# A two-layer hybrid block on one core: more weight buffers, earlier small rows, and 256-column products in pairs

## The chip, the cores and the metric

One core of one Trainium2 chip. The metric is the device time of one execution in microseconds. The kernel before was run three times: 1761.48, 1764.64 and 1771.3 us, median 1764.64.

## The reference, cut to what matters

Two layers over 256 latent and 256 context tokens of width 1024 (the context tokens read only context tokens). All arithmetic is float32.

```python
for l in range(2):
    xn = adaln(x, norm1, ...)            # RMS norm, then scale and shift made from c by w_mod
    p  = xn @ w_in                       # columns: cq 384, ckv 256, kr 32, sq 512, sk 128, sv 128,
                                         #          qkv 1536, z 512, a/b 32, gates 3072
    ya = latent attention(cq, ckv, kr)   # 8 heads, w_uq, w_ukv
    yb = window attention(sq, sk, sv)    # 8 heads on 2 key heads, with sinks
    yc = gated DeltaNet, both directions(qkv, a, b) * silu(z)
    y  = (sig(g0)*(ya@w_pa) + sig(g1)*(yb@w_pb) + sig(g2)*(yc@w_pc)) @ w_out
    x  = x + m2 * y
    h  = dwconv(adaln(x, norm2, ...) @ ffn_up); a, b = split(h)
    x  = x + m5 * ((silu(a) * b) @ ffn_down)
return rmsnorm(x, norm_f)
```

In layer 1 the context's outputs are not wanted any more. There cq, sq, z, the gates and all that follows the mixers are computed for the 256 latent tokens alone, while keys and values are still computed for all 512.

## The kernel before, in words

Activations lie transposed in SBUF: features on the partitions, tokens along the free axis, so a product has a 128x128 block of weights as its stationary operand and 512 (layer 0) or 256 (layer 1, latent tokens alone) moving columns. Float32 accuracy comes from two parts. `load_split` (L181) loads up to 512 KB of weights (four row blocks of 256 columns, here called a weight part) into a tile raw, casts it on ACT to a first part wh (L189), and on DVE takes the difference raw - wh as a low part wl (`split_L`, L177). `mm3` (L197) then does three matmuls for each block: wh with the activation's first part, wh with its low part, wl with its first part (L199, L200, L201). The pools have `NRAW` = 3 buffers of raw, `NWH` = 3 of wh and `NWL` = 4 of wl (P, L88 to L93, and L1648). Modulation matrices (`mod_part`, L583) are loaded into raw buffers too, in layer 0's mixers, and used by PE without a split (L593).

`linear` (L274) computes a product in units of 256 output columns, two tiles of 128. A unit takes two PSUM banks (2 KB each, so 512 float32 columns) from the pool mm, which has three, or g, which has five. It goes through the weight parts in order, and within a part through the two column tiles; after the last part each tile is evicted by its own operation.

The order of the work is written by a planner in the kernel. Generators yield estimated microseconds; `chain` (L1391) runs the dependent chains (DeltaNet tables, decay, solve, scan, attention) and after each step `fill` (L214) spends the credit on queued products, the fill work. The queue ends with the gate products (`gates`, L1370): each is evicted through a Sigmoid (L1376), stored to DRAM by a DMA that ACT issues (L1377), and loaded again in the merge (L1515); gates that were not reached ahead are computed in the merge itself (L1531). A scheduler of the framework then orders the instructions of each engine by priority and by buffers that come free. Each engine's queue runs in that order, and an instruction that waits holds up those behind it. Nearly all loads are issued by SP.

`load_vectors` (L538) collects small vectors (biases, norms, convolution taps) as rows of one tile, by nine DMAs, and transposes them on PE. For layer 0 they are issued by POOL at the start, for layer 1 by SP just before layer 0's attention (L1465), where `load_conv` (L561) does the same with the MLP's taps of both layers, by two DMAs each. These use b2 tiles of 2 KB, as the attention does.

Stages of layer 0, about, in us: products for DeltaNet keys 26 to 90, decay, solve and scan to 360, preparation of the attentions to 407, attentions to 510, merge and output product to 700, MLP to 1070. Layer 1: mixers to 1390, attentions to 1470, merge to 1530, MLP to 1750.

Of the kernel before, what the change touches and what calls it, by code (L numbers as in the profile page):

```python
# [14 lines left out]
D = 1024  # L15
# [14 lines left out]
def make_consts():  # L30
# [61 lines left out]
    bx=4, wd=0, dc=1, gk=(0, 0), hpe=60, w_t=5, w_k=3, w_s=0, w_r=1.5, w_n=3, w_o=4.0, nr=3, nh=3, nl=4, nb2=7, st=0, ab=(0.0, 0.0, 0.0, 0.0),  # L92
# [42 lines left out]
class Kernel:  # L135
# [138 lines left out]
    def linear(self, w, k0, nk, c0, ncol, X, evac, cols=None, kgrp=4, split=None, hook=None, gate=False):  # L274
# [5 lines left out]
        for u0 in range(0, ncol, 256):  # L280
# [5 lines left out]
            pss = [self.ps([128, T], "g" if self.wide and self.unit % 2 else "mm") for _ in range(nt)]  # L286
# [11 lines left out]
            def products(kg, wt, cs):  # L298

                g, H, L = wt  # L300
                for i in range(nt):
                    due = g
                    for k in range(g):
                        cc = slice(i * 128, i * 128 + 128)
                        self.mm3(pss[i][:, cs[i]], H[:, k, cc], L[:, k, cc], XH[kg + k][:, cs[i]], XL[kg + k][:, cs[i]],
                                 kg + k == 0, kg + k == nk - 1)
                        if hk:
                            hk["n"] += 1
                            if hk["n"] in self.P["hk"]:
                                next(hk["g"])  # L310
                        elif k % self.P["ly"] == self.P["ly"] - 1 and k < g - 1:
                            yield (cs[i].stop - cs[i].start) * self.P["ly"] * 3 / 2400
                            due -= self.P["ly"]
                    if kg + g == nk:
                        with self.tc.high_priority(self.P["hpe"]):
                            evac(u0 // 128 + i, pss[i], cs[i])
                    yield (cs[i].stop - cs[i].start) * due * 3 / 2400
# [13 lines left out]
            cs = [cols(u0 // 128 + i) if cols else slice(0, T) for i in range(nt)]  # L331
            for kg in range(0, nk, kgrp):
                yield from products(kg, load(kg), cs)
# [204 lines left out]
    def load_vectors(self, l):  # L538

        nc, i = self.nc, self.ins  # L540
        q = nc.gpsimd if l == 0 else nc.sync
        ident = self.con("ident")
        rows = self.b2([128, 128])
        for nm, (r0, n) in VEC_ROWS.items():
            if nm == "gdn_norm":
                for h in range(2):
                    q.dma_start(out=rows[r0:r0 + 1, h * 64:h * 64 + 64], in_=i[nm][l:l + 1, :])
                continue
            a = i[nm] if nm == "norm_f" else i[nm][l]
            if nm == "gdn_conv":  # L550
                a = a.rearrange("t (r c) -> (t r) c", c=128)
            else:
                a = a.rearrange("(r c) -> r c", c=128)
            q.dma_start(out=rows[r0:r0 + n, :], in_=a)
        for a, b in ((0, 56), (56, NVEC)):
            yield
            ps = self.ps([128, T], "g")
            nc.tensor.transpose(ps[:, :b], rows[:b, :], ident[:b, :b])
            nc.vector.tensor_copy(self.vec[l][:, a:b], ps[:, a:b])

    def load_conv(self, l):  # L561
# [735 lines left out]
    def layer(self, l):  # L1297
# [25 lines left out]
        def proj_cq():  # L1323
            cq = A["cq"] = self.b4([128, 3, n]) if last else self.s8([128, 3, n])
            yield from self.linear(w, 0, KD, C_CQ, 384, X, lambda t, p, cs: self.evac(t, cq[:, t, :], p[:, cs]), cols=c_o)
# [6 lines left out]
        def proj_sq():  # L1332
# [4 lines left out]
            for u in range(2):  # L1337
                self.gsync()
                pss = [self.ps([128, T], "mm") for _ in range(2)]
                for kg in range(0, KD, 4):  # L1340
# [6 lines left out]
                    H, L = self.load_split(pieces, [128, 4, 256])  # L1347
                    for j in range(2):
# [6 lines left out]
                    yield 5.1 * len(streams) / 2  # L1355

        def proj_z():
            if not last:
                A["zs"] = self.s8([128, 4, n])
            zs = A["zs"]  # L1360

            def evz(t, p, cs):
                nc.scalar.activation(out=zs[:, t, :], in_=p[:, cs], func=AF.Silu)

            yield from self.linear(w, 0, KD, C_Z, 512, X, evz, cols=c_o)
# [4 lines left out]
        def gates():  # L1370

            for bi, (gi, _) in enumerate(gate_br):
                for u in range(4):
                    def ev(t, p, cs, bi=bi, u=u):
                        sg = self.b2([128, T])[:, :n]
# [4 lines left out]
                    yield from self.linear(w, 0, KD, C_GATE + gi * D + u * 256, 256, X, ev, cols=c_o, gate=True)  # L1380
# [339 lines left out]
```

## Time and profile before

| | |
|---|---|
| runs | 1761.48, 1764.64, 1771.3 us; median 1764.64 |
| profiled execution | 1760.08 us, its span 1758.3 us |
| mean granted TensorE clock | 0.976 |
| busy: PE / PE's weight loads / DVE / ACT / POOL | 95% / 77% / 66% / 44% / 12% |
| instructions | 31525 |
| HBM read, written | 213.85 MB, 11.80 MB; mean 130 GB/s |

PE is TensorE's matmuls, PEld its weight loads, DVE VectorE, ACT ScalarE, POOL GpSimd, SP SyncE. A q behind an engine's name marks its sequencer, which issues DMAs. L and a number is a line of the kernel. `out<-in` names tiles without their buffer numbers. An arrow in brackets behind an idle time names what ended it.

### The profile page before, as it was taken

Reading aid. Unit: us, or ns where it says so; the run is one execution under the profiler, and the core shown is the slowest. Engines: PE = TensorE matmul, PEld = TensorE weight load, DVE = VectorE, ACT = ScalarE, POOL = GpSimd, SP = SyncE. Lnnn points to the kernel's source line nnn. Section 1 sums busy time; section 2 is a strip of 40 time slices with the busy share of each in tenths; the row PEclk is TensorE's granted clock in tenths of the full one; section 3 lists DMA queues with packets and bytes.
Section 4 is the critical chain, followed back from the end, with each engine's and each line's share of the span. In section 5 each row is a group of like instructions: output and inputs, shape, how many; then the busy total and the mean of one; then the engine's idle time right before and its main releaser. Section 6 shows DMA issues by size and latency. Waiting matters only on the chain. (4 is left out here: it accounts for less than half of the span.)

```text
span 1758.3 us, 31525 instructions
## 1 busy us (share of the span) xinstructions
PE 1668.4 (95%) x12723; PEld 1355.3 (77%) x12723; DVE 1160.7 (66%) x2223; ACT 777.4 (44%) x1377; POOL 217.0 (12%) x217
## 2 busy tenths in 40 slices
PE   6989998998999999999999999989988899999997
PEld 3768766775557888668888888778887667999997
DVE  3888697675775534545435553699997877667684
ACT  3664412234665233324324433465532575556463
POOL 1000000002100312011001111020302301212010
PEclk9999998998999999999999999999897999999999
DMA  9424335333135533853233343434351223745663
GB/s 348 118 59 122 103 100 172 74 87 101 55 102 175 185 124 105 313 186 101 87 105 96 96 157 109 126 90 132 103 130 38 61 85 107 235 145 178 185 186 123
DMA packets 216944, 228.75 MB, mean 130 GB/s; under 512 B 51228, under 2 KB 195422, under 8 KB 215646
## 3 DMA queue, kind: packets, MB, share of 16 engines
q1 hardware_dynamic: 211582, 220.11, 40.9%
q10 hardware_dynamic: 4928, 6.56, 1.0%
q8 instruction: 100, 1.64, 0.4%
q14 instruction: 46, 0.38, 0.1%
q0 software_dynamic: 288, 0.06, 0.0%
HBM read 213.85 MB, written 11.80 MB: 128 GB/s over the span
## 5 line engine op out<-in xcount | busy, mean ns | idle before, releaser
L179 DVE TENSOR_TENSOR wl<-raw,wh 128x1024 fp32r<-128x1024 f32 (+2 forms) x294 | 357.7, 1217 | 236.9 <-ACT wh L189 235.7
L189 ACT CAST wh<-raw 128x1024 fp32r<-128x1024 f32 (+2 forms) x294 | 298.6, 1018 | 382.3 <-PE mm L200 187.6
L199 PE MATMUL mm<-xnh,wh 128*128 128x512 f32 (+2 forms) x1072 | 378.6, 354 | 4.6 <-DVE s L131 1.9
L201 PE MATMUL mm<-xnh,wl 128*128 128x512 f32 (+2 forms) x1072 | 373.2, 351 | 5.0 <-DVE wl L179 4.9
L200 PE MATMUL mm<-xnl,wh 128*128 128x512 f32 (+2 forms) x1072 | 374.4, 350 | 0.0
L199 PEld LDWEIGHTS mm<-xnh,wh 128*128 128x128 f32 (+1 forms) x1072 | 204.8, 191 | 39.2 <-issue 7.7
L201 PEld LDWEIGHTS mm<-xnh,wl 128*128 128x128 f32 (+1 forms) x1072 | 204.3, 191 | 35.6 <-DVE wl L179 7.0
L200 PEld LDWEIGHTS mm<-xnl,wh 128*128 128x128 f32 (+1 forms) x1072 | 204.8, 191 | 27.6 <-issue 4.0
L199 PE MATMUL g<-xnh,wh 128*128 128x256 f32 (+1 forms) x496 | 167.6, 340 | 1.4 <-ACT xnh L405 1.4
L200 PE MATMUL g<-xnl,wh 128*128 128x256 f32 (+1 forms) x496 | 166.3, 337 | 0.2 <-DVE xnl L406 0.2
L201 PE MATMUL g<-xnh,wl 128*128 128x256 f32 (+1 forms) x496 | 166.3, 337 | 0.0
L199 PE MATMUL mm<-s,wh 128*128 128x256 f32 (+1 forms) x458 | 149.4, 328 | 0.7 <-DVE s L534 0.6
L201 PE MATMUL mm<-s,wl 128*128 128x256 f32 (+1 forms) x458 | 149.3, 327 | 0.6 <-DVE wl L179 0.6
L200 PE MATMUL mm<-s,wh 128*128 128x256 f32 (+1 forms) x458 | 149.1, 326 | 0.1
L1620 POOL TENSOR_TENSOR b<-b,b 128x512 f32<-128x512 f32 (+1 forms) x44 | 54.4, 1237 | 442.1 <-DVE b L1604 381.1
L199 PEld LDWEIGHTS g<-xnh,wh 128*128 128x128 f32 x496 | 94.7, 192 | 15.0 <-issue 3.3
L201 PEld LDWEIGHTS g<-xnh,wl 128*128 128x128 f32 x496 | 94.7, 191 | 10.5 <-issue 1.2
L199 PE MATMUL g<-s,wh 128*128 128x512 f32 (+1 forms) x304 | 102.7, 338 | 0.0
L200 PEld LDWEIGHTS g<-xnl,wh 128*128 128x128 f32 x496 | 94.7, 191 | 10.1 <-DVE xnl L406 0.8
L200 PE MATMUL g<-s,wh 128*128 128x512 f32 (+1 forms) x304 | 102.2, 336 | 0.0
L201 PE MATMUL g<-s,wl 128*128 128x512 f32 (+1 forms) x304 | 102.1, 336 | 0.0
L199 PEld LDWEIGHTS mm<-s,wh 128*128 128x128 f32 x458 | 86.8, 190 | 8.8 <-DVE s L534 1.1
(290 smaller groups left out, 2699.0 us busy)
## 6 DMA issues: line engine op xcount, KB each, us to landing
raw<-in_w_in_dram SPq DMA_DIRECT2D x92, 512.0 KB
raw<-in_ffn_up_dram SPq DMA_DIRECT2D x80, 512.0 KB
s<-in_w_mod_dram SPq DMA_DIRECT2D x64, 512.0 KB
raw<-in_w_mod_dram SPq DMA_DIRECT2D x32, 512.0 KB
raw<-in_ffn_down_dram SPq DMA_DIRECT2D x32, 512.0 KB
raw<-in_w_out_dram SPq DMA_DIRECT2D x16, 512.0 KB
raw<-in_ffn_down_dram SPq DMA_DIRECT2D x16, 384.0 KB
spill<-s SPq DMA_DIRECT2D x4, 1024.0 KB
```

The costliest lines, as they stand in the source:

```text
L179: self.nc.vector.tensor_tensor(out=out, in0=x, in1=h.bitcast(F32), op=ALU.subtract)
L189: nc.scalar.copy(H, raw)
L199: mm(ps, lhsT=wH, rhs=xH, start=start, stop=False)
L200: mm(ps, lhsT=wH, rhs=xL, start=False, stop=False)
L201: mm(ps, lhsT=wL, rhs=xH, start=False, stop=stop)
L1620: nc.gpsimd.tensor_tensor(out=y[:, cs], in0=y[:, cs], in1=av[t][:, cs], op=ALU.mult)
```

## The change

It raises `nr` (raw) from 3 to 5 and `nh` (wh) from 3 to 4, and makes room for that by a smaller scratch area for the descriptors of POOL's DMAs. It issues layer 1's small rows and the taps of both layers on SP right after layer 0's spill of x, into row buffers of their own; their transposes stay where they were. In layer 1 the products of cq, sq, z and the gates that are computed ahead use one PSUM bank per unit: two tiles of 256 columns side by side. For that all weight parts of a unit are loaded and split first, then the first column tile is accumulated through all parts, then the second, and one operation evicts both; a gate unit is stored by one DMA in place of two. The gates computed in the merge, the MLP and layer 0's products keep two banks.

```diff
-    ... nr=3, nh=3, nl=4, nb2=7 ...
+    ... nr=5, nh=4, nl=4, nb2=7 ...
...
-    def linear(self, w, k0, nk, c0, ncol, X, evac, cols=None, kgrp=4, split=None, hook=None, gate=False):
+    def linear(self, w, k0, nk, c0, ncol, X, evac, cols=None, kgrp=4, split=None, hook=None, gate=False, pair=False):
...
-            pss = [self.ps([128, T], "g" if self.wide and self.unit % 2 else "mm") for _ in range(nt)]
+            tag = "g" if self.wide and self.unit % 2 else "mm"
+            if pair:
+                bank = self.ps([128, 2, S], tag)
+            else:
+                pss = [self.ps([128, T], tag) for _ in range(nt)]
...
-                    if kg + g == nk:
+                    if kg + g == nk and (not pair or i == nt - 1):
                         with self.tc.high_priority(self.P["hpe"]):
-                            evac(u0 // 128 + i, pss[i], cs[i])
+                            if pair:
+                                evac(u0 // 128, bank[:, :nt], cs[i])
+                            else:
+                                evac(u0 // 128 + i, pss[i], cs[i])
...
+            if pair:
+                wts = [(kg, load(kg)) for kg in range(0, nk, kgrp)]
+                for i in range(nt):
+                    for kg, wt in wts:
+                        yield from products(kg, wt, cs, (i,))
+                continue
...
-        rows = self.b2([128, 128])
+        rows = self.b2([128, 128]) if l == 0 else self.sb([128, 128], "rows", F32, 3)
+        if l:
+            self.rows = rows
+            for j in range(DEPTH):
+                q.dma_start(out=rows[NVEC + 4 * j:NVEC + 4 * j + 4, :], in_=i["ffn_conv"][j].rearrange("t (r c) -> (t r) c", c=128)[128:132, :])
...
-        f0, f1 = self.b2([128, 128]), self.b2([128, 128])
+        f0, n = self.sb([128, 128], "rows", F32, 3), NVEC + 4 * DEPTH
         nc.sync.dma_start(out=f0, in_=fr[0:128, :])
-        nc.sync.dma_start(out=f1[:4, :], in_=fr[128:132, :])
+        yield
         ps = self.ps([128, T], "g")
         nc.tensor.transpose(ps[:, :128], f0, ident)
-        nc.tensor.transpose(ps[:, 128:132], f1[:4, :], ident[:4, :4])
-        nc.vector.tensor_copy(self.fcv[l], ps[:, :132])
+        nc.tensor.transpose(ps[:, 128:128 + n], self.rows[:n, :], ident[:n, :n])
+        nc.vector.tensor_copy(self.fcv[l][:, :128], ps[:, :128])
+        nc.vector.tensor_copy(self.fcv[l][:, 128:132], ps[:, 128 + NVEC + 4 * l:132 + NVEC + 4 * l])
...
                     def ev(t, p, cs, bi=bi, u=u):
+                        if last:
+                            sg = self.b2([128, 2, S])
+                            nc.scalar.activation(out=sg, in_=p, func=AF.Sigmoid)
+                            nc.scalar.dma_start(out=gate_in[:, bi, 2 * u:2 * u + 2], in_=sg)
+                            gate_n[1] += 1
+                            return
...
+        if l == 0:
+            small = [self.load_vectors(1)] + [self.load_conv(j) for j in range(DEPTH)]
+            for g in small:
+                next(g)
...
-            for _ in self.load_vectors(1):
-                pass
-            for j in range(DEPTH):
-                self.load_conv(j)
+            for g in small:
+                for _ in g:
+                    pass
...
-    nc = bacc.Bacc("TRN2", target_bir_lowering=False, num_devices=1)
+    nc = bacc.Bacc("TRN2", target_bir_lowering=False, num_devices=1, dynamic_dma_scratch_size=2048)
```

`proj_cq`, `proj_z` and `gates` pass `pair` in layer 1; `proj_sq` does the same by hand, with its four matmul blocks of a part kept until both column tiles are through. cq and sq alternate between ACT and DVE by unit where they did by tile.

## Rows read from the trace of the kernel before

**Rows 1.** The page, busy time of the engines (share of the span, instructions).

```profile
PE 1668.4 (95%) x12723; PEld 1355.3 (77%) x12723; DVE 1160.7 (66%) x2223; ACT 777.4 (44%) x1377; POOL 217.0 (12%) x217
```

**Rows 2.** Waits of PE, whole run: total us, times, longest us.

```profile
PE mm L593 <- DMA raw<-in_w_mod_dram: 6.6, 6, 2.8
...
PE mm L201 <- DVE wl L179: 5.6, 5, 3.5
...
PE mm L199 <- DVE s L131: 1.9, 1, 1.9
...
PE mm L199 <- ACT wh L189: 0.9, 1, 0.9
```

**Rows 3.** Stretches: length, busy us (instructions) by engine, granted clock, DMA share, GB/s.

```profile
core 0: us, PE busy (x) PEld busy (x) DVE busy (x) ACT busy (x) POOL busy (x), PEclk, DMA share, GB/s
110.00:121.00 11.00, 7.45 (x32) 5.26 (x32) 10.93 (x14) 6.70 (x9) 1.04 (x2) 1.00 0.14 49
121.00:125.00 4.00, 4.00 (x12) 3.12 (x11) 2.82 (x21) 0.45 (x1) 0.00 (x0) 0.57 0.48 131
...
250.00:267.00 17.00, 13.87 (x275) 8.67 (x274) 15.16 (x44) 0.60 (x1) 0.00 (x0) 1.00 0.69 230
267.00:272.00 5.00, 4.61 (x82) 3.20 (x83) 3.26 (x7) 1.41 (x4) 0.00 (x0) 0.66 0.80 273
...
414.00:425.00 11.00, 9.55 (x36) 5.42 (x37) 5.09 (x19) 4.28 (x11) 0.93 (x1) 0.53 0.55 178
...
1144.00:1320.00 176.00, 162.43 (x1804) 143.21 (x1804) 166.01 (x331) 90.41 (x153) 32.80 (x31) 0.96 0.43 112
...
1500.00:1540.00 40.00, 40.00 (x336) 40.00 (x335) 24.77 (x33) 21.59 (x33) 10.25 (x10) 1.00 0.72 238
```

**Rows 4.** PE in order of time, 384 to 425 us: start, us, instruction [idle before].

```profile
413.04 0.64 PE L593 MATMUL mm<-raw,cT 128*32 128x256 f32 x8 [2.82 <-DMA raw<-in_w_mod_dram]
...
414.95 0.42 PE L558 MATMUL g<-cst,b 114*128 114x114 f32 x1 [1.07 <-DMA b<-in_gdn_norm_dram]
...
416.55 0.45 PE L570 MATMUL g<-cst,b 128*128 128x128 f32 x1 [0.38 <-DVE fcv L572]
```

**Rows 5.** SP in order of time, whole run, equal issues merged.

```profile
3.06 0.60 SPq L186 DMA_DIRECT2D raw<-in_w_in_dram  x1
3.70 15.89 SPq L458 DMA_DIRECT2D s<-in_w_mod_dram  x14
...
44.42 28.08 SPq L186 DMA_DIRECT2D raw<-in_w_in_dram  x7
...
395.86 12.72 SPq L591 DMA_DIRECT2D raw<-in_w_mod_dram  x2
408.62 0.44 SPq L554 DMA_DIRECT2D b<-in_b_mod_dram  x1
...
415.19 0.25 SPq L568 DMA_DIRECT2D b<-in_ffn_conv_dram  x1
```

**Rows 6.** Waits of ACT, whole run.

```profile
ACT wh L189 <- PE mm L200: 187.6, 87, 7.9
```

**Rows 7.** Waits of SP's queue, whole run.

```profile
SPq L591 <- PE mm L593: 95.5, 18, 26.1
```

**Rows 8.** DVE in order of time, 112 to 121 us.

```profile
115.14 3.93 DVE L131 STREAM_TRANSPOSE s<-s 32x1024 f32<-32x1024 f32 x2
...
119.18 1.22 DVE L179 TENSOR_TENSOR wl<-raw,wh 128x1024 fp32r<-128x1024 f32 x1
```

**Rows 9.** ACT's groups by form, whole run: count, busy us, mean ns, idle before.

```profile
L1376 ACT ACTIVATE b<-mm 128x512 f32<-128x512 f32 x16 | 9.5, 597 | 12.4 <-PE mm L201 11.4 <-PE g L939 1.0
...
L1376 ACT ACTIVATE b<-mm 128x256 f32<-128x256 f32 x18 | 6.6, 382 | 5.8 <-PE mm L201 5.7
```

**Rows 10.** DMA issues: count, KB each, median us to landing.

```profile
b<-in_norm_dram POOLq DMA_DIRECT2D x2, 4.0 KB, 5.4
```

**Rows 11.** PE in order of time, 44 to 50 us.

```profile
45.28 0.26 PE L558 MATMUL g<-cst,b 114*128 114x114 f32 x1
```

More of the change, by code (lines that the diff above doesn't have):

```diff
@@ L91 @@
     lag=(0, 0, 2, 4, 5), nmod=(2, 5), hk=(5, 12), f0=(1.0, 1.6, 1.0, 1.0, 1.5, 1.0, 1.0), f1=(1.0, 1.0, 1.0, 0.3, 1.0, 1.0, 0.3), lat=1.0,
-    bx=4, wd=0, dc=1, gk=(0, 0), hpe=60, w_t=5, w_k=3, w_s=0, w_r=1.5, w_n=3, w_o=4.0, nr=3, nh=3, nl=4, nb2=7, st=0, ab=(0.0, 0.0, 0.0, 0.0),
+    bx=4, wd=0, dc=1, gk=(0, 0), hpe=60, w_t=5, w_k=3, w_s=0, w_r=1.5, w_n=3, w_o=4.0, nr=5, nh=4, nl=4, nb2=7, st=0, ab=(0.0, 0.0, 0.0, 0.0),
     st2=6, bge=2, hpa=40, hpn=0, hpk=40, hpv=40)
@@ L296, in load, with products @@
                 return (g,) + self.load_split(pieces, [128, g, uw])
-            def products(kg, wt, cs):
+            def products(kg, wt, cs, tiles=None):
                 g, H, L = wt
-                for i in range(nt):
+                for i in tiles or range(nt):
                     due = g
@@ L304, in products @@
                         cc = slice(i * 128, i * 128 + 128)
-                        self.mm3(pss[i][:, cs[i]], H[:, k, cc], L[:, k, cc], XH[kg + k][:, cs[i]], XL[kg + k][:, cs[i]],
+                        self.mm3(bank[:, i] if pair else pss[i][:, cs[i]], H[:, k, cc], L[:, k, cc], XH[kg + k][:, cs[i]], XL[kg + k][:, cs[i]],
                                  kg + k == 0, kg + k == nk - 1)
@@ L1324, in proj_cq @@
             cq = A["cq"] = self.b4([128, 3, n]) if last else self.s8([128, 3, n])
-            yield from self.linear(w, 0, KD, C_CQ, 384, X, lambda t, p, cs: self.evac(t, cq[:, t, :], p[:, cs]), cols=c_o)
+            if last:
+                yield from self.linear(w, 0, KD, C_CQ, 384, X, lambda t, p, cs: self.evac(t // 2, cq[:, t:t + p.shape[1], :], p), cols=c_o, pair=True)
+                return
+            yield from self.linear(w, 0, KD, C_CQ, 384, X, lambda t, p, cs: self.evac(t, cq[:, t, :], p[:, cs]))
         def alloc_zsq():
@@ L1338, in proj_sq @@
                 self.gsync()
-                pss = [self.ps([128, T], "mm") for _ in range(2)]
+                pss = [self.ps([128, T], "mm") for _ in range(1 if last else 2)]
+                wts = []
                 for kg in range(0, KD, 4):
@@ L1347, in proj_sq @@
                     H, L = self.load_split(pieces, [128, 4, 256])
+                    if last:
+                        wts.append((H, L))
+                        continue
                     for j in range(2):
@@ L1354, in proj_sq @@
                             self.evac(j, sq[:, 2 * u + j, :], pss[j][:, oc])
-                    yield 5.1 * len(streams) / 2
+                    yield 5.1
+                for j in range(2 if last else 0):
+                    for k in range(KD):
+                        H, L = wts[k // 4]
+                        self.mm3(pss[0][:, j * S:j * S + S], H[:, k % 4, j * 128:j * 128 + 128], L[:, k % 4, j * 128:j * 128 + 128],
+                                 XH[k][:, oc], XL[k][:, oc], k == 0, k == KD - 1)
+                    if j:
+                        self.evac(u, sq[:, 2 * u:2 * u + 2, :], pss[0].rearrange("p (j c) -> p j c", j=2))
+                    yield 2.56
         def proj_z():
@@ L1362, in evz @@
             def evz(t, p, cs):
-                nc.scalar.activation(out=zs[:, t, :], in_=p[:, cs], func=AF.Silu)
-            yield from self.linear(w, 0, KD, C_Z, 512, X, evz, cols=c_o)
+                nc.scalar.activation(out=zs[:, t:t + 2, :] if last else zs[:, t, :], in_=p if last else p[:, cs], func=AF.Silu)
+            yield from self.linear(w, 0, KD, C_Z, 512, X, evz, cols=c_o, pair=last)
         gate_in, gate_br = self.dram.tile([128, 3, 8, n], F32, name=f"gates{l}"), ((2, "c"), (0, "a"), (1, "b"))
@@ L1374, in ev @@
                     def ev(t, p, cs, bi=bi, u=u):
+                        if last:
+                            sg = self.b2([128, 2, S])
+                            nc.scalar.activation(out=sg, in_=p, func=AF.Sigmoid)
+                            nc.scalar.dma_start(out=gate_in[:, bi, 2 * u:2 * u + 2], in_=sg)
+                            gate_n[1] += 1
+                            return
                         sg = self.b2([128, T])[:, :n]
@@ L1379, in gates @@
                     gate_n[0] += 1
-                    yield from self.linear(w, 0, KD, C_GATE + gi * D + u * 256, 256, X, ev, cols=c_o, gate=True)
+                    yield from self.linear(w, 0, KD, C_GATE + gi * D + u * 256, 256, X, ev, cols=c_o, gate=True, pair=last)
         def push(*gens):
```

## The prediction

> **What bounds the kernel now.** I read the page first, for the busiest engine: PE is busy 1668.4 of 1758.3 us [rows 1], so all that can be had without removing matmuls is 1758.3 - 1668.4 = 90 us of idle time, plus what slow clock costs. The change removes no matmul. Second, the waits of PE over the whole run, to see which of that idle time a deeper supply of weights could end. Four rows matter [rows 2]: 6.6 us for the modulation matrices (tile raw), 5.6 us for the low halves wl, 1.9 us and 0.9 us before the first matmul of a product. The other waits of PE are for links of the DeltaNet and softmax chains, which the change does not touch. Third, the table of stretches around the longest of these waits [rows 3]: after each of them the granted clock of the next few microseconds is 0.57, 0.66 and 0.53 of full speed, that is, mostly the lower of the two levels, 1.2 GHz. A wait costs its idle time and a slow stretch behind it. Fourth, the queues that feed PE: ACT's wait list says that the cast to wh is held up mostly by PE's last use of an older wh, 187.6 us in 87 waits [rows 6]; SP's says that modulation loads wait 95.5 us for PE to give back a raw buffer [rows 7]. So wh and raw are the short buffers; idle time there costs PE nothing until it surfaces in [rows 2].
>
> **Part 1: five raw and four wh buffers.** Taken by stretch, against the profiled execution (1758.3 us span, 1760.08 us in all).
>
> (a) Start of the layer-0 attention. SP issues one modulation load at about 396 us and the next only when PE has freed a buffer, just before 408.62; PE starts on it at 413.04, after 2.82 us idle [rows 4, 5]. With two more buffers that load goes out with the earlier ones. Then PE waits 1.07 us for the small rows and 0.38 us behind their eviction [rows 4]; with the rows loaded 370 us earlier the first goes, and the second goes too, as the four transposes no longer wait for loads one by one. Idle: 2.82 + 1.07 + 0.38 = 4.3. In 414 to 425 us PE is busy 9.55 us at clock 0.53 [rows 3]; at full clock that is 9.55 x 0.47 = 4.5 us less. I take 4.0, since some of the drop may come anyhow. DVE is busy only 5.09 of those 11 us, so nothing else bounds. Sum 8.3.
>
> (b) Layer-0 scan, 250 to 272 us. The other raw waits are 6.6 - 2.8 = 3.8 us [rows 2, 4], and the slow stretch after them costs 4.61 x 0.34 = 1.6 us [rows 3]. But DVE is busy 15.16 of 17 us there: PE that arrives sooner will partly wait for the scan's next DVE result. That is what is late next. I take half of 5.4: 2.7.
>
> (c) wl. Its longest wait, about 3.5 us, has its reason in DVE's order: the split stands behind 3.93 us of stream transposes and starts at 119.18 [rows 2, 8]. With a fourth wh the cast, and so the split, can be ordered a weight part earlier. Idle 5.6 us, slow clock 4.00 x 0.43 = 1.7 us [rows 2, 3], together 7.3. DVE has 10.93 of 11 us full there, but what PE waited with was fill work that nobody's chain needs. I take two thirds: 4.9.
>
> (d) The 0.9 us for wh [rows 2] is in the dense layer-0 MLP: 0.9.
>
> DVE and ACT do as many casts and splits as before.
>
> **Part 2: early small rows.** Thirteen SP issues leave 408.62 to 415.44 us, where they cost the above, for the place behind the spill, before the raw loads at 44.42 us [rows 5]. They take SP up to 6.8 us there. PE and ACT do not stand behind them: only the weight loads do, and those seven loads spend 28.08 us at SP because raw buffers are full [rows 5], so the delay is covered as long as three (now five) parts lie ahead. Bounds 0 to +6.8; I take 0, nearest to that row. Two small evictions for one per layer on DVE: under 1 us beside other work, 0. The rows' own 512-byte buffers free five b2 tiles at the attention's start: 0.
>
> The descriptor scratch shrinks to 2048 bytes. The trace shows no wait for it. Nine row loads on POOL land up to 5.4 us after issue [rows 10]; one after another from 1.3 us they would end near 50, and PE wants the last at 45.28 [rows 11]: bounds 0 to +4.6. They are small and now overlap, so 0. At the start one raw load goes ahead of fourteen modulation loads that take 15.89 us, 1.14 each [rows 5]; two more raw buffers may let two more ahead: 0 to +2.3. The order of the first is kept by the queue, not by lack of buffers, so 0.
>
> **Part 3: pairs in layer 1.** Gates done ahead (18 evictions, so 9 units), z, cq and sq, 2 units each: 15 units. Matmuls stay. A Sigmoid takes 382 ns on 256 columns and 597 on 512 [rows 9]: 9 x (2 x 382 - 597) = 1.5 us off ACT, and 9 fewer stores, all off the path. A unit takes one of three mm banks instead of two, which can end the 1.9 us wait for an evicted bank [rows 2]. Against it, the first column tile must be finished before the second starts, so the second weight part is wanted after half a column tile's products. PE does 336 matmuls in 40 us in a full stretch [rows 3], 0.119 us each; a part of one tile is 12 of them, 1.43 us, where until now both tiles' 24, 2.86 us, came first. Between: -1.9 to +15 x 1.43 = +21.5 us. I take -1.0: casts and splits run ahead of PE, and the waits for wl are 5.6 us in the whole run, of which 3.5 us are one wait in layer 0 [rows 2].
>
> Here the Trainium skill speaks against the change: "PSUM — Partial Sum Buffer", section "The four PSUM rules", says that two accumulation groups open in one bank spoil each other when the second starts, so a shared bank forces the groups one after the other. No row here shows two in one bank; if every unit paid for that order in full, the sum would be 16.8 - 21.5, a loss of 4.7 us.
>
> **Sum:** 8.3 + 2.7 + 4.9 + 0.9 + 1.0 = 17.8 us. The profiled execution lies 4.6 us (0.26%) under the median of 1764.64, so 1742 for its like, and 1764.6 - 17.8 = 1747 for the median.
>
> **Rivals.** *The buffers only park more loads.* A modulation load keeps its buffer until PE uses it, and SP is one queue: five full buffers block it like three. For it: 95.5 us of such waits [rows 7], and DVE full beside (b) and (c). Against: in (a) one more buffer is all that is missing. Then only (a) stays, 4.3 to 8.3 us: 1756 to 1760, say 1758, no change that shows. A measurement of this kernel tells about 0.5% (8.8 us) from none.
>
> *Slower: the pairs starve PE.* Place: the layer-1 stretch 1144 to 1320 us, where DVE is busy 166.01 of 176 us [rows 3]. There a split that is wanted 1.43 us sooner is not made sooner, since wl stays at four buffers and DVE has no room. Price: per unit 1.43 us if it just comes late, or about 3.5 plus 1.7 of slow clock if it falls behind a transpose, as in (c). With eight of the units in that stretch at 3.9 on average, 31 us against the 16.8 of the other terms and more: 1764.6 + 15 = 1780. It decides from (16.8 + 8.8) / 8 = 3.2 us a unit on. Against: wh, the shorter buffer, gets deeper.
>
> *More than forecast.* Casts that wait for PE hold ACT's queue [rows 6], and with it the Exp and Square that chains stand behind. In 1144 to 1320 us PE idles 176 - 162.43 = 13.6 us and loses 162.43 x 0.04 = 6.5 to the clock [rows 3]; with two thirds of these 20 gone, 1747 - 13 = 1734. Against: DVE, not ACT, is full there.
>
> **How the numbers follow.** Forecast 0.48, parked loads 0.24, pairs starve 0.13, more 0.15. The forecast's own bounds: all of (a) to (d) and the bank wait, 8.8 + 5.4 + 7.3 + 0.9 + 1.9 = 24, gives 1740; the costs of part 2, 6.8 + 4.6 + 2.3, would take most of the gain back: 1761. The range runs from half of the "more" case, 1733, over parked loads to 1766; outside lie the starved pairs and some of "more", 0.2. Faster: 0.15 and all but 0.01 of 0.48, 0.62; same 0.25; slower 0.13.
>
> **What would show it.** Right: the waits for raw and wl in PE's list fall from 12.2 us to under 4; in the attention's first 15 us there is no modulation or row wait, and its clock is 1.0; modulation loads wait for PE as long as before, but two loads further ahead. (b) is wrong if the scan's waits for DVE grow by what raw gives back. Part 3 is right if L201's waits in layer 1 stay under 1 us, and wrong if they come near 10. Part 2 is wrong if the first 80 us get longer. The whole is wrong if the layer-0 waits are gone and the span is not shorter: then the chains set it.

## The result, and the profile after

The change makes the kernel faster: 1742.05 us, the median of four runs (1739.98 to 1744.14), against 1767.97 us for the kernel before on the same chip (1761.48 to 1773.14); ratio 0.9863, 95% interval 0.9839 to 0.9886. The profiled execution of after spans 1738.9 us. That of before (1758.3, its own time 1760.08) lies below all the timed runs of before, so the profiles differ by 19.4 us where the medians differ by 25.9. All that follows accounts for the 19.4.

The page of after, busy time (answers to [rows 1]), and the waits of PE over the whole run (answers to [rows 2]; total us, times, longest us; L955 is now L974, L593 L612, L1098 L1117):

```profile
PE 1663.4 (96%) x12723; PEld 1356.9 (78%) x12723; DVE 1162.7 (67%) x2224; ACT 771.9 (44%) x1360; POOL 211.1 (12%) x217
```

```profile
PE g L974 <- DVE b L963: 7.8, 8, 1.5
...
PE mm L201 <- DVE wl L179: 2.8, 2, 2.3
...
PE mm L612 <- DMA raw<-in_w_mod_dram: 2.2, 4, 0.8
...
PE g L1117 <- ACT s L194: 2.0, 1, 2.0
```

The waits for raw and wl are down from 12.2 to 5.0 us, and 2.3 of these 5.0 are one new wait. The wait for DVE in the scans of both layers (L974) has grown from 5.0 to 7.8 us; by windows it fell in layer 0's scan, from 3.5 to 3.0, and rose in layer 1's, from 1.5 to 4.9.

Where the 19.4 us went is read from the table of stretches, with the same six stages cut in both kernels: to the last scan product of layer 0 (A), to the last value product of its attention (B), to the last residual after its MLP (C), to layer 1's last scan product (D), its last value product (E), and the end (F). Columns are the stretch, its length, busy time and instructions of PE, PEld, DVE, ACT, POOL, granted clock, DMA share, GB/s. Before:

```profile
0.00:354.10 354.10, 325.07 (x3222) 243.52 (x3222) 258.06 (x534) 140.06 (x241) 14.09 (x25) 0.98 0.45 136
354.10:551.90 197.80, 185.44 (x1038) 121.86 (x1032) 135.26 (x375) 114.54 (x270) 21.33 (x25) 0.96 0.32 95
551.90:1098.00 546.10, 544.24 (x2771) 441.71 (x2770) 259.97 (x350) 186.05 (x263) 74.48 (x61) 1.00 0.43 141
1098.00:1364.30 266.30, 242.32 (x2856) 210.10 (x2857) 228.82 (x459) 121.17 (x217) 42.21 (x39) 0.94 0.39 103
1364.30:1476.80 112.50, 102.53 (x659) 71.76 (x655) 84.01 (x213) 71.11 (x155) 18.73 (x22) 0.98 0.24 71
1476.80:1758.30 281.50, 268.77 (x2199) 266.31 (x2197) 194.60 (x294) 144.50 (x232) 46.13 (x45) 0.98 0.57 175
```

After:

```profile
0.00:351.50 351.50, 325.90 (x3221) 245.00 (x3221) 258.48 (x535) 138.57 (x240) 14.10 (x25) 0.97 0.46 141
351.50:541.60 190.10, 183.22 (x1042) 121.41 (x1037) 134.84 (x377) 114.20 (x270) 20.92 (x25) 0.97 0.31 100
541.60:1084.20 542.60, 541.26 (x2767) 441.10 (x2766) 260.86 (x350) 185.96 (x263) 75.84 (x61) 1.00 0.43 140
1084.20:1350.60 266.40, 243.55 (x2859) 210.75 (x2858) 228.66 (x458) 117.63 (x204) 41.18 (x39) 0.93 0.39 106
1350.60:1458.60 108.00, 101.33 (x655) 72.66 (x650) 84.25 (x212) 70.64 (x153) 18.51 (x22) 0.97 0.25 74
1458.60:1738.90 280.30, 268.14 (x2199) 266.04 (x2197) 195.57 (x293) 144.93 (x231) 40.52 (x45) 0.98 0.55 171
```

PE's instructions are the same stage by stage to within four (a few records are missing, and a few matmuls move across a cut), so the lengths may be compared: A gains 2.6 us, B 7.7, C 3.5, E 4.5, F 1.2, and D loses 0.1. The gain around the start of layer 0's attention is as forecast. The first 81 us are longer, and layer 1's attention is shorter; neither was in the sum.

### The profile page after: what moved, and what is told of

It reads as the page before. It is cut to its first block, busy times and chain, and to the rows that moved or that the text cites. A ratio compares the mean times of both kernels' runs of the same rounds, so it can differ in the third digit from the quotient of the medians.

```text
span 1738.9 us, 31515 instructions
## 1 busy us (share of the span) xinstructions
PE 1663.4 (96%) x12723; PEld 1356.9 (78%) x12723; DVE 1162.7 (67%) x2224; ACT 771.9 (44%) x1360; POOL 211.1 (12%) x217
## 4 chain that ended last, share of the span: by engine, by line
PE 77%; DVE 13%; issue 4%; DMA 3%; ACT 2%; POOL 0%; SPq 0%; POOLq 0%; DVEq 0%; ACTq 0%
PE mm L199 13%; PE mm L200 12%; PE mm L201 12%; PE g L199 8%; PE g L200 8%; PE g L201 8%; DVE s L131 3%; PE g L1070 2%; PE g L1133 2%; DVE wl L179 2%; PE g L1117 2%; DMA s<-in_w_mod_dram 2%; DVE sm L131 1%; PE g L612 1%; PE g L974 1%
## 5 line engine op out<-in xcount | busy, mean ns | idle before, releaser
L199 PE MATMUL mm<-xnh,wh 128*128 128x512 f32 (+2 forms) x1072 | 378.8, 355 | 4.6 <-DVE s L131 2.0
L1663 POOL TENSOR_TENSOR b<-b,b 128x512 f32<-128x512 f32 (+1 forms) x44 | 49.6, 1128 | 444.1 <-DVE b L1647 391.8
```

The costliest lines, as they stand in the source:

```text
L199: mm(ps, lhsT=wH, rhs=xH, start=start, stop=False)
L1663: nc.gpsimd.tensor_tensor(out=y[:, cs], in0=y[:, cs], in1=av[t][:, cs], op=ALU.mult)
```

## The experiments

Twelve kernels: first each part alone, then parts taken out of the change, then the pairs taken apart. The table has the length of each stage in us, from windows cut at the same instructions as above, and the time against the kernel before on the same chip.

| kernel | A | B | C | D | E | F | median us | ratio to before, 95% |
|---|---|---|---|---|---|---|---|---|
| before | 354.1 | 197.8 | 546.1 | 266.3 | 112.5 | 281.5 | | |
| after | 351.5 | 190.1 | 542.6 | 266.4 | 108.0 | 280.3 | 1742.05 | 0.9863 (0.9839 to 0.9886) |
| 1 buffers alone | 346.4 | 199.3 | 542.9 | 266.3 | 121.1 | 280.5 | 1758.26 | 0.9966 (0.9950 to 0.9982) |
| 2 early rows alone | 352.7 | 190.6 | 546.4 | 265.7 | 116.0 | 281.5 | 1754.72 | 0.9949 (0.9924 to 0.9974) |
| 3 pairs alone | 353.5 | 199.9 | 546.3 | 271.6 | 112.1 | 281.2 | 1766.20 | 1.0022 (0.9999 to 1.0046) |
| 4 no pairs | 353.4 | 189.8 | 542.6 | 268.7 | 118.3 | 280.4 | 1753.19 | 0.9940 (0.9918 to 0.9962) |
| 5 no early rows | 347.1 | 200.2 | 542.3 | 266.6 | 108.2 | 280.3 | 1746.74 | 0.9902 (0.9884 to 0.9920) |
| 6 raw 5, wh 3 | 353.9 | 189.9 | 545.2 | 268.8 | 114.9 | 281.0 | 1754.71 | 0.9947 (0.9927 to 0.9966) |
| 7 raw 3, wh 4 | 355.3 | 196.4 | 541.4 | 264.7 | 107.9 | 280.9 | 1748.10 | 0.9896 (0.9870 to 0.9922) |
| 8 rows later | 346.9 | 191.6 | 542.4 | 267.4 | 107.9 | 280.5 | 1738.47 | 0.9856 (0.9834 to 0.9878) |
| 9 two evictions | 351.0 | 190.1 | 542.3 | 267.9 | 107.2 | 280.1 | 1740.37 | 0.9861 (0.9833 to 0.9888) |
| 10 order, two banks | 351.7 | 192.8 | 542.2 | 272.7 | 113.8 | 280.0 | 1752.10 | 0.9924 (0.9899 to 0.9949) |
| 11 gates unpaired | 350.6 | 190.0 | 542.9 | 273.8 | 113.5 | 280.4 | 1752.19 | 0.9925 (0.9900 to 0.9951) |
| 12 rows later, wh 5 | 350.3 | 190.6 | 539.9 | 275.6 | 111.5 | 283.7 | 1746.80 | 0.9896 (0.9869 to 0.9923) |

A row of stages is one execution. After and runs 4, 9, 10 and 11 have the same code up to layer 1, and their A, B and C spread over 2.8, 3.0 and 0.7 us, so a smaller difference in one stage shows nothing. The profiled executions of runs 12, 10 and 4 lie 6.6, 2.9 and 1.8 us above their medians, that of before 4.3 us below its median beside runs 1 to 4 (1764.39): the verdicts rest on the ratios.

### Each part alone

**Run 1, the buffers alone** (against before):

```diff
-    ... nr=3, nh=3, nl=4 ...
+    ... nr=5, nh=4, nl=4 ...
-    nc = bacc.Bacc("TRN2", target_bir_lowering=False, num_devices=1)
+    nc = bacc.Bacc("TRN2", target_bir_lowering=False, num_devices=1, dynamic_dma_scratch_size=2048)
```

> The kernel before with five raw and four wh buffers (and the smaller descriptor scratch that makes room), nothing else. Theory (the buffers carry the gain): 12 to 20 us faster than before; layer 0's scores start 7 to 13 us earlier, since the 2.82 us modulation wait and most of the slow clock behind it go while the 1.07 us row wait stays; the wl waits at 115 to 121 us go; the tables end where they ended before. Rival 'parked loads': 4 to 8 us, all of it at the start of layer 0's attention. Rival 'the pairs bring the late gain': what is gained by the end of layer 1's scan is all there is, so the attention and merge of layer 1 take as long as before.

Measured: ratio 0.9966, about 6 us, the size that the parked loads would give, but not in their place. A gains 7.7 us and C 3.2; B, where the forecast had its largest term, gains nothing; E loses 8.6. At the attention's start PE still waits 1.7 us for a modulation load and 1.4 us for the rows. PE's row there (start, length, ..., [idle before <- what ended it]) and SP's timeline (start, length, operation, count) show why:

```profile
405.07 0.64 PE L593 MATMUL mm<-raw,cT 128*32 128x256 f32 x8 [1.68 <-DMA raw<-in_w_mod_dram]
```

```profile
363.50 19.45 SPq L591 DMA_DIRECT2D raw<-in_w_mod_dram  x5
...
400.55 0.33 SPq L591 DMA_DIRECT2D raw<-in_w_mod_dram  x1
400.92 0.43 SPq L554 DMA_DIRECT2D b<-in_b_mod_dram  x1
...
407.58 2.46 SPq L591 DMA_DIRECT2D raw<-in_w_mod_dram  x5
```

The load that PE waits for is the sixth. Five had gone out from 363.50 us on and filled the five buffers; the sixth went out at 400.55 us, after SP had waited 17.0 us for PE to give a buffer back. That is what the parked loads would do. Five more loads then stand behind the rows, 6.6 us in SP's queue, but PE waits for none of them: the 1.7 us are all its waiting for modulation in B.

**Run 2, the early rows alone** (against before, which keeps three buffers each; the scratch is as in after):

```diff
+        if l == 0:
+            small = [self.load_vectors(1)] + [self.load_conv(j) for j in range(DEPTH)]
+            for g in small:
+                next(g)
...
-            for _ in self.load_vectors(1):
-                pass
-            for j in range(DEPTH):
-                self.load_conv(j)
+            for g in small:
+                for _ in g:
+                    pass
```

> The kernel before with the small rows issued early (and the smaller scratch), three raw and three wh buffers, no pairs. Theory: the thirteen early issues hold up the weight loads behind them, so the tables end 2.6 to 7 us later (worse than the 2.6 us with five raw buffers); the row wait of 1.07 us and the 0.38 us behind it go at the attention's start, where the 2.82 us modulation wait stays. In all 1 us faster to 5 us slower. Rival (my own forecast, rows cost nothing): 0 to 3 us faster, the first 90 us unchanged.

Measured: about 9 us faster, beyond what either side expected. B is 190.6 us, as in after, with three raw buffers. So most of the gain at the attention's start is the rows': run 1 has the buffers and not the gain, run 2 the gain and not the buffers. But part of the modulation wait stays with three raw, in run 2 and in run 7 below, and is nearly gone in after (PE's rows of run 2, run 7 and after):

```profile
412.01 0.64 PE L598 MATMUL mm<-raw,cT 128*32 128x256 f32 x8 [1.36 <-DMA raw<-in_w_mod_dram]
```

```profile
414.70 0.64 PE L612 MATMUL mm<-raw,cT 128*32 128x256 f32 x8 [1.50 <-DMA raw<-in_w_mod_dram]
```

```profile
410.60 0.62 PE L612 MATMUL mm<-raw,cT 128*32 128x256 f32 x2 [0.25 <-DMA raw<-in_w_mod_dram]
```

In all of these, before and run 1 included, the load waited for is the one that SP could issue only when PE had given back its first modulation buffer (at 408.25, 400.55, 406.93, 409.48 and 405.66 us in before, runs 1, 2, 7 and after), and PE goes on 4.5 to 5.2 us after that issue. What differs is how long PE has other work before it wants the load: 2.0 us in before, 2.8 in run 1, 3.7 in runs 2 and 7, 4.7 in after. Two more buffers give it two more loads to multiply with, some 0.9 us. With early rows it does their transposes and the first scores in that time, some 1.8 us, where in run 1 these stand behind the wait.

**Run 3, the pairs alone** (against before: `pair` in `linear`, `proj_cq`, `proj_sq`, `proj_z` and `gates` as in the change, nothing else).

> The kernel before with the pairs alone, three raw and three wh buffers. Theory: nothing changes until layer 1; its mixers take 2 us less to 4 us more, the total is within 4 us of before. Rival 'pairs starve PE': 10 to 30 us slower, with waits for wl of 10 us or more in 1144 to 1320 us, since here no deeper wh helps. Rival 'the pairs bring the late gain': layer 1's attention and merge take about 6 us less and the total is 4 to 8 us less.

Measured: 1.0022, no change that shows. D takes 5.3 us more, E 0.4 less. Neither starved to a price of 10 us nor a gain of 6.

**Run 4, after without the pairs** (against after):

```diff
-                    yield from self.linear(w, 0, KD, C_GATE + gi * D + u * 256, 256, X, ev, cols=c_o, gate=True, pair=last)
+                    yield from self.linear(w, 0, KD, C_GATE + gi * D + u * 256, 256, X, ev, cols=c_o, gate=True)
...
```

with the same for cq, sq and z.

> The kernel after without the pairs (buffers and early rows stay). Theory: within 2 us of the kernel after, so about 22 to 27 us faster than before. Rival 'pairs starve PE': 2 to 10 us faster than the kernel after, as the 1.6 us that layer 1's mixers lost come back. Rival 'the pairs bring the late gain': 4 to 8 us slower than the kernel after, lost in layer 1's attention and merge.

Measured: 0.9940, so 0.8% slower than after, most of it in E (118.3 against 108.0). The theory fell. Pairs that are worth nothing alone are worth over 10 us when the buffers are there.

### Parts taken out

**Run 5, after with the rows where they were** (the early block and the `rows` tile undone).

> The kernel after with the small rows issued where they were before, at the attention's start (buffers and pairs stay). Theory: the tables end 2 to 3 us earlier than in the kernel after and the 2.3 us wait for wl near 65 us goes; the row waits of 1 to 2 us come back at the attention's start, with 0 to 4 us of slow clock. In all within 3 us of the kernel after. Rival (rows cost nothing early): 2 to 6 us slower than after, since only the attention's start differs.

Measured: 0.9902, some 7 us slower than after. A is 4.4 us shorter than in after, B 10.1 us longer: the early rows cost the one and bring the other. The theory had the first right and the second too small. SP in after, from the spill on:

```profile
37.75 3.27 SPq L1459 DMA_DIRECT2D spill<-s  x2
41.07 2.00 SPq L561 DMA_DIRECT2D rows<-in_ffn_conv_dram  x2
...
49.12 0.83 SPq L585 DMA_DIRECT2D rows<-in_ffn_conv_dram  x2
50.05 3.33 SPq L186 DMA_DIRECT2D raw<-in_w_in_dram  x5
```

The raw loads behind the rows start at 50.05 us where they started at 44.42 [rows 5], and PE then idles 2.31 us for wl at 64.77 us, a wait that was not there before.

**Run 6 and run 7, one of the two buffers** (against after):

```diff
-    ... nr=5, nh=4, nl=4 ...
+    ... nr=5, nh=3, nl=4 ...
```

> The kernel after with three wh buffers in place of four (five raw stay). Theory: the modulation wait at the attention's start stays away (that is raw), but the wl waits at 115 to 121 us come back, 3 to 7 us, and the 0.9 us for wh in the MLP; 4 to 10 us slower than after. Rival (raw alone carries it): within 2 us of after.

```diff
-    ... nr=5, nh=4, nl=4 ...
+    ... nr=3, nh=4, nl=4 ...
```

> The kernel after with three raw buffers in place of five (four wh stay). Theory: the 2.82 us modulation wait and the slow clock behind it come back at layer 0's attention, and the early rows are no longer covered at all, so the tables end 3 to 6 us later than in the kernel after; in all 8 to 14 us slower than after. Rival 'wh alone carries it': within 3 us of after.

Measured: without the fourth wh 0.9947, without the two raw 0.9896, against 0.9863 for after. The first is some 15 us slower than after, beyond the theory's 10, the second about 6, short of its 8. In the stretch from layer 0's decay tables to its first scan product (run 6 first, then run 7)

```profile
80.40:225.30 144.90, 140.50 (x1072) 111.31 (x1071) 116.38 (x238) 81.75 (x132) 2.07 (x4) 0.99 0.31 95
```

```profile
83.20:221.40 138.20, 135.63 (x1058) 107.49 (x1057) 114.69 (x236) 77.69 (x127) 2.07 (x4) 1.00 0.31 96
```

three wh take 144.9 us and four 138.2 (before 143.9, after 139.1), with 2.8 us of wl waits in run 6 and 0.9 in run 7: it is wh that ends them. Of the modulation wait of 2.82 us, which I gave to raw, 1.50 us come back with three raw at the same place, and 1.62 us at another in B, which takes 196.4 us in place of 190.1. Run 2, with early rows, three raw and three wh, took 190.6; why B takes 6 us more with the fourth wh stays open.

**Run 8, the rows later** (against after):

```diff
-        if l == 0:
-            small = [self.load_vectors(1)] + [self.load_conv(j) for j in range(DEPTH)]
-            for g in small:
-                next(g)
         self.mark(f"gtab_{l}")
...
         self.mark(f"gscan_{l}_0")
+        if l == 0:
+            small = [self.load_vectors(1)] + [self.load_conv(j) for j in range(DEPTH)]
+            for g in small:
+                next(g)
         alloc_zsq()
```

> The kernel after with the block that issues the small rows moved from behind the spill to the start of layer 0's scan, near 220 us, nothing else. Theory: the weight loads of the first 90 us are no longer behind thirteen issues, so the tables end 2 to 3 us earlier and the 2.3 us wait for wl near 65 us goes; the attention starts as well fed as in the kernel after; in all 2 to 5 us faster than after. Rival: the scan's chain, not the fill, sets the end of layer 0's mixers, or the issues cost as much there; within 1 us of after.

Measured: 0.9856, the lowest of all kernels here, though its interval covers that of after: whether it beats after stays open. A is 346.9 us, 4.6 less than in after, as with no early rows, and B 191.6, as with them. The queue order is not quite what I had written. The framework sends the rows out from 64.38 us on, between raw loads, and not near 220:

```profile
38.22 3.30 SPq L1459 DMA_DIRECT2D spill<-s  x2
41.62 4.50 SPq L186 DMA_DIRECT2D raw<-in_w_in_dram  x3
...
64.38 0.75 SPq L561 DMA_DIRECT2D rows<-in_ffn_conv_dram  x2
```

By then the raw loads that the first products want are out, and the same issues cost nothing that shows.

### The pairs taken apart

After run 4 the question was what in a pair works, and only with four wh: the shared bank, the single eviction, or the order.

**Run 9, a shared bank, two evictions** (against after, gates shown; cq, sq and z alike):

```diff
-                                evac(u0 // 128, bank[:, :nt], cs[i])
+                                for j in range(nt):
+                                    evac(u0 // 128 + j, bank[:, j], cs[i])
...
-                            sg = self.b2([128, 2, S])
+                            sg = self.b2([128, T])[:, :n]
                             nc.scalar.activation(out=sg, in_=p, func=AF.Sigmoid)
-                            nc.scalar.dma_start(out=gate_in[:, bi, 2 * u:2 * u + 2], in_=sg)
+                            nc.scalar.dma_start(out=gate_in[:, bi, 2 * u + t], in_=sg)
```

> The kernel after, where each pair still shares a bank and is computed tile by tile, but is evicted by two operations of 256 columns, and a gate unit stored by two DMAs. In the runs so far the products' 4.5 us gain at layer 1's attention (90.1 us before, 84.2 after, 94.1 to 96.8 with the buffers alone) came only with pairs and four wh together. Theory (the shared bank does it: more units can be in flight): layer 1's attention stays at 83 to 86 us, the total within 3 us of after. Rival (the one eviction does it, less work in ACT's queue): the attention goes back to 89 to 97 us, 5 to 12 us slower than after.

**Run 10, the pairs' order, two banks** (against after):

```diff
-            if pair:
-                bank = self.ps([128, 2, S], tag)
-            else:
-                pss = [self.ps([128, T], tag) for _ in range(nt)]
+            pss = [self.ps([128, T], tag) for _ in range(nt)]
...
-                    if kg + g == nk and (not pair or i == nt - 1):
+                    if kg + g == nk:
```

> The kernel after with the pairs' order (all weight parts loaded, then the first column tile through all of them, then the second), but each tile in a bank of its own with its own eviction. Theory (the bank does it): the attention of layer 1 goes back to 89 to 97 us and the total is 5 to 12 us slower than after. Rival (the order does it, since the loads and casts of a unit are all asked for ahead of its products): the attention stays at 83 to 86 us, the total within 3 us of after.

**Run 11, gates unpaired** (against after: `pair=last` taken from the gates alone).

> The kernel after with the gates as before, cq, sq and z still in pairs. Theory (the gates are the fill of layer 1's attention): the attention goes back to 89 to 97 us, 5 to 12 us slower than after. Rival (the pairs of cq, sq and z end the mixers in another state, and the attention follows from that): within 3 us of after, the attention at 83 to 86 us.

Measured: run 9 is after again (0.9861; E 107.2). Run 10 has lost it (0.9924; E 113.8, the attention proper, from its own first products on PE to its last value product, 90.2 us against 84.2), and so has run 11 (0.9925; E 113.5, attention 91.4). Neither the one eviction nor the order nor the pairs of cq, sq and z do it; what it takes is the gates' shared bank. The forecasts of the theory held in all three. Whether the gates' pairs would do without those of cq, sq and z was not run.

How a bank does it is seen in layer 1's attention. The chain comes to a place where PE must wait for ACT (the profile names a cast to s, L194), and only fill matmuls can cover that. I count those into mm banks from the end of the scan: up to the first value product, and from there to the idle time. Run 10, and under it its rows of PE around the place (start, length, ..., [idle before <- what ended it]) and its first Sigmoid on ACT after the scan:

```profile
1359.40:1402.50 43.10, 26.01 (x138) 20.93 (x138) 3.90 (x8) 3.76 (x9) 0.96 0.25 74
1402.50:1415.90 13.40, 2.47 (x16) 2.06 (x16) 0.00 (x0) 0.00 (x0) 1.00 0.12 39
```

```profile
1411.47 0.28 PE L201 MATMUL mm<-xnh,wl 128*128 128x256 f32 x1
1415.96 0.63 PE L1111 MATMUL g<-cst,b 128*128 128x128 f32 x4 [4.21 <-ACT s L194]
...
1426.10 0.39 PE L199 MATMUL mm<-xnh,wh 128*128 128x256 f32 x1 [0.30 <-ACT b L1403]
```

```profile
1425.66 0.38 ACT L1403 ACTIVATE b<-mm 128x256 f32<-128x256 f32 x1
```

After, the same:

```profile
1350.60:1394.10 43.50, 26.71 (x137) 21.66 (x137) 3.76 (x7) 3.76 (x9) 0.92 0.25 74
1394.10:1407.60 13.50, 4.64 (x34) 4.22 (x34) 0.00 (x0) 0.00 (x0) 1.00 0.13 39
```

```profile
1405.31 0.28 PE L201 MATMUL mm<-xnh,wl 128*128 128x256 f32 x1
1407.64 0.63 PE L1117 MATMUL g<-cst,b 128*128 128x128 f32 x4 [2.04 <-ACT s L194]
...
1413.99 0.36 PE L199 MATMUL mm<-xnh,wh 128*128 128x256 f32 x1
```

```profile
1418.17 0.60 ACT L1411 ACTIVATE b<-mm 128x512 f32<-128x512 f32 x1
```

In run 10 fill stops after 138 + 16 = 154 matmuls and goes on at 1426.10, released by the Sigmoid (L1403) that empties a bank; the last 16 do not cover the wait, and PE idles 4.21 us. In after 137 + 34 = 171 come before the place, the wait is 2.04 us, and fill goes on at 1413.99, 4 us before ACT's first Sigmoid after the scan. In the same count run 1 has 138 + 16 = 154 and before 107 + 45 = 152:

```profile
1364.30:1405.40 41.10, 19.27 (x107) 15.26 (x107) 3.94 (x8) 3.78 (x9) 1.00 0.23 65
1405.40:1418.40 13.00, 5.96 (x45) 5.54 (x45) 0.00 (x0) 0.00 (x0) 1.00 0.27 83
```

So with two banks a unit some 153 is the end, whatever the wh buffers. The other runs agree: with two banks 152 in run 2 and 154 in runs 4 and 11, and in all six such kernels fill goes on 0.2 to 0.8 us after the start of a Sigmoid; with a shared bank and four wh 171 in runs 5, 7 and 8 and 166 in run 9, and fill goes on before one. The fourth wh lets 31 of them run earlier, and they are missing later where they covered the wait: 3.68 us in run 1, where before waits 1.58 us, for DVE. With a shared bank 17 more can be ahead. With three wh the pairs do not help: runs 3 and 6 have 101 + 31 = 132, and go on before a Sigmoid, so it is not a bank that fill lacks there; that it is a cast is likely, but no wait names it.

The wait at this place is not the whole of the 8.6 us that the buffers alone lose in E. PE idles 9.6 us in E in run 1 and 10.0 in before, so what is lost is busy time, 111.5 us against 102.5, at a granted clock of 0.89 against 0.98. And run 10, with the same 154 and a longer wait, takes only 1.3 us more than before. How much of the slow clock stands right behind the wait is seen in the last section.

Over D and E together, 4 wh and two banks for a gate unit give 386.5 to 387.4 us (runs 1, 4, 10, 11), 4 wh and a shared bank 372.6 to 375.3 (after, runs 5, 7, 8, 9), and 3 wh 378.8 to 383.7 (before, runs 2, 3, 6). D's share is not explained by the count above: in layer 1's scan runs 1, 4, 10 and 11 have a wait of PE for DVE of 4.7 to 4.9 us, where no kernel with 4 wh and a shared bank waits longer than 2.4 us at once. How the banks lead to it was not followed.

**Run 12, rows later, four raw and five wh** (against run 8):

```diff
-    ... nr=5, nh=4, nl=4 ...
+    ... nr=4, nh=5, nl=4 ...
```

> The kernel after with the small rows issued at the start of layer 0's scan (as in the run with the rows later) and with four raw and five wh buffers in place of five and four. Theory (wh is the short buffer outside the modulation, and raw is worth 5 us only in layer 0's attention, where three gave 140.7 us and five 135.9): the layer-0 attention loses 0 to 2.5 us, the stretch from the tables to the scan and the MLP gain 0 to 3; within 3 us of the run with the rows later, so 22 to 29 us faster than before. Rival (raw is what the modulation needs): 3 to 6 us slower than that run.

Measured: 0.9896, some 7 us slower than run 8, more than theory and rival allowed. In the one profiled execution, itself 6.6 us above the median, C gains 2.5 us and B 1.0, but A and F take 3.4 and 3.2 more, D 8.2 and E 3.6 (D and E together 387.1 us, with a shared bank). It is not the banks at the place above: there the waits for ACT are down to 1.06 and 0.68 us. Of D's 8.2 us 7.0 are busy time of PE for the same matmuls, at a clock of 0.91 against 0.94. What brings the clock down there stays open.

## Why the prediction was right, and where it was not

The forecast was 17.8 us and a median of 1747; the profiles differ by 19.4, the medians by 25.9, and 1742.05 lies inside the range of 1733 to 1766. The total is right with much of its composition wrong: that it came so close is in part luck.

- **(a), layer 0's attention start, 8.3 us.** Size and place right: B gains 7.7, the granted clock behind the start is 1.00 where it was 0.53 [rows 3], and one raw wait of 0.3 us is left. The cause was in the main wrong. "With two more buffers that load goes out with the earlier ones" failed in run 1: five loads fill five buffers as three fill three, and the next one waits for PE as before. With the buffers alone B gains nothing, with the early rows alone 7.2 us. The rows' own waits went, as written; that their early transposes and the first scores would also cover the load's flight was not in the text, and the buffers add only some 0.9 us to that cover.
- **(b), scan, 2.7 us.** Nothing that shows: from the first to the last scan product layer 0 takes 131.0 us where it took 131.4. PE's waits in this stretch, before and after:

```profile
PE g L955 <- DVE b L944: 3.5, 3, 1.4
PE mm L593 <- DMA raw<-in_w_mod_dram: 3.2, 4, 1.2
```

```profile
PE g L974 <- DVE b L963: 3.0, 2, 1.5
PE mm L612 <- DMA raw<-in_w_mod_dram: 2.0, 3, 0.8
```

Only 3.2 of the 3.8 us that I had counted lie here, and 2.0 of them stayed. The step that failed is that two more raw buffers end these waits. Other short waits took the place of the 1.2 us that went (all waits for DVE together 4.9 us where they were 4.4), and PE idles 9.9 us where it idled 9.2.
- **(c), wl, 4.9 us.** Right, cause too: 143.9 to 139.1 us from the tables to the scan, and runs 6 and 7 give it to wh. The clock of 110 to 125 us is 1.00 in after.
- **(d), MLP, 0.9 us.** Under-sized: C gains 3.5 us, 2.6 of them in the MLP. The runs give it to wh: C takes 545.2 to 546.4 us with three, 541.4 to 542.9 with four and 539.9 with five. Only 0.5 of the 2.6 is idle time; the rest is PE's busy time for the same matmuls at a granted clock of 1.00, and no row says why.
- **Part 2, taken as 0 within 0 to 6.8.** The step that failed is "the delay is covered as long as three (now five) parts lie ahead": at 41 us there is room for loads that run 8 issues from 41.62 us on, and in after these stand behind the rows until 50.05. Cost 4.4 us in A (after against run 5) or 7.0 (run 4 against run 1; pairs act in layer 1 alone, so these measure one cost twice), and nothing beside three buffers (run 2). The first 80 us got longer, as the text had named for this case. Against it stands most of the gain of (a).
- **Part 3, -1.0 within -1.9 to +21.5.** The good end was too short: I priced a freed bank by one wait of 1.9 us that I took for its sign, and that wait is still there, with 2.0 us. Over D and E the shared bank is worth 12.6 us beside four wh (after against run 4) and nothing beside three. The waits for wl in layer 1 stayed under 1 us, as I had written. A loss that I had not seen, 8.6 us from the buffers alone in E, hides in between: the 4.4 us gained in D and E are what is left of both.

The bad end of part 3 rested on the order. The Trainium skill, "PSUM — Partial Sum Buffer", section "The four PSUM rules", says that the first matmul of a second group, where it is flagged as a start, makes a group still open in the same bank lose its sum; it also names ways round this, which the kernel does not use. No run here has two open groups in one bank. Every group here has that flag, so a shared bank forces the order, and paid for in full it would have lost 4.7 us. Run 10 has the forced order without the bank: 0.9924, against 0.9940 for run 4, which has neither. The order by itself costs nothing that shows in the time, though PE waits 3.7 us for wl in run 10's D, where run 4 has no such wait.

Of the rivals, parked loads gives run 1's time but by another way (a gain in A and C, less a loss in E), though its mechanism is what run 1 shows at the attention's start. The pairs did not starve PE. "More than forecast" had its gain in layer 1's mixers, and D takes 266.4 us where it took 266.3. Of the signs of being right, one was missed: the waits for raw and wl fell to 5.0 us, not under 4.

## What to carry to other kernels

A late load has two possible causes, a buffer that is not free and an issue that stands behind others in its queue; find the load that the engine waits for, and what its queue waited for before issuing it, before buying buffers. Here it was a buffer, and still two more of them helped less than other work put where the load was on its way, as each new buffer was filled by one more load. Buffers of successive stages (raw, wh, PSUM banks) work as one chain: deepen one, and fill work runs ahead until the next is full, and is then missing where it used to cover a wait, so count how many matmuls can be ahead and test buffers together with what follows them. Loads moved early should go behind the first loads that PE is about to want, not in front of them.

## What was not expected of the hardware

An idle time of PE can cost nearly as much again behind it. In run 1 the 3.68 us wait at the place above was followed by this (stretch by stretch):

```profile
1408.30:1412.00 3.70, 0.04 (x1) 0.07 (x2) 3.52 (x10) 3.60 (x11) 1.72 (x1) 0.87 0.00 0
1412.00:1418.00 6.00, 6.00 (x22) 3.10 (x23) 3.51 (x8) 0.79 (x2) 0.00 (x0) 0.51 0.26 88
1418.00:1432.00 14.00, 14.00 (x92) 9.89 (x91) 6.60 (x16) 10.08 (x19) 0.00 (x0) 1.00 0.15 46
1432.00:1442.00 10.00, 10.00 (x39) 7.65 (x40) 5.20 (x12) 3.55 (x9) 0.00 (x0) 0.66 0.28 96
...
1448.00:1456.00 8.00, 8.00 (x34) 4.60 (x32) 3.53 (x11) 3.80 (x11) 0.00 (x0) 0.57 0.00 0
```

In the 6 us behind the wait the clock is 0.51, nearly all at the lower level, 1.2 GHz. After the 2.04 us wait of after it stayed at 1.00:

```profile
1405.60:1407.60 2.00, 0.00 (x0) 0.00 (x0) 1.92 (x5) 1.88 (x6) 1.61 (x1) 1.00 0.00 0
1407.60:1413.90 6.30, 6.26 (x37) 3.72 (x38) 6.12 (x13) 2.99 (x5) 0.00 (x0) 1.00 0.27 86
```

The other kernels do the same. Where the wait is 3.68 to 4.21 us (runs 4, 10, 11), the 6 us behind it run at 0.50, 0.72 and 0.76; where it is 2.05 or 2.06 us (runs 5, 7, 8, 9), at 1.00.

Over E the granted clock is 0.89 in run 1 with 111.53 us busy, and 0.97 with 101.33 us in after: a difference of 10.2 us of busy time for the same matmuls, where the idle times (9.6 and 6.7 us) differ by 2.9. The stretch behind the wait is some 2.9 us of it (6.00 x 0.49). Most of the rest lies in the two slow stretches further down (10.00 x 0.34 and 8.00 x 0.43, 3.4 us each). Before the first of these PE had been busy for 14 us without a break, so it is not behind an idle time, and why the clock falls there stays open.
